# Stick-breaking attention: q and k projected with stationary weights, and the product for the second 512-key chunk on GpSimd

## The chip, the cores and the metric

The kernel runs on one core of one Trainium2 chip. The metric is the device time of one execution in microseconds. Engines are named as in the profile: PE is TensorE (PEld its weight loads), DVE VectorE, ACT ScalarE, POOL GpSimd, SP SyncE, whose queue issues nearly all transfers.

## What is computed

One block of a transformer trunk over 2048 positions of width 1024: RMS norm, one combined projection, two kinds of attention side by side (four heads of differential attention, eight heads of stick-breaking attention), an output projection with a residual, and a SwiGLU feed-forward part with a residual. The change is in stick-breaking attention alone:

```python
def stick_breaking_attention(q, k, v):
    """q, k, v: (B, S, H, D). A[t,s] = beta_ts * prod_{s<j<t}(1 - beta_tj), s < t."""
    ...
        z = jnp.einsum('bqhd,bkhd->bhqk', qb, k).astype(jnp.float32) * scale
        mask = (k_pos[None, :] < q_pos[:, None])[None, None]
        log_1mb = jnp.where(mask, jax.nn.log_sigmoid(-z), 0.0)
        rem = lax.cumsum(log_1mb, axis=3, reverse=True) - log_1mb
        a = jnp.where(mask, jnp.exp(jax.nn.log_sigmoid(z) + rem), 0.0)
        return jnp.einsum('bhqk,bkhd->bqhd', a.astype(v.dtype), v)
```

Here S = 2048, a head has D = 64, and the inputs are float32. The kernel gets more than float16 precision out of float16 matmuls by splitting each operand into a high and a low part (hi = float16 of the value, lo = float16 of the rest) and adding the products hi·hi, hi·lo and lo·hi.

## The kernel before

**Stages.** The work is cut into eight groups g. Groups 0 to 3 are one differential head each (two maps), groups 4 to 7 two stick-breaking heads each (m = 0, 1). The projection of a group is a stream of 16 tiles of 128 positions; it is written out ahead of the group's attention, mixed into the attention of the group before (`advance` says how many tiles must have been written by which step). A scheduler then gives each engine a fixed order from a simulated timeline and priorities (`pri`); the projection's matmuls ("pm") have a lower one than scores and values. While the last group runs there is no projection left, and the output projection (L761) takes its place. After that comes the feed-forward part, which the change does not touch. Where a function can use one of several engines, `pick` takes the one with the least load noted so far (`note`).

**Projection of a tile** (`proj_tile`, L314). The normalized and transposed inputs xt of a tile are the stationary operand, 128 x 128 at a time, and 384 columns of weights are the moving one (128 for q, 128 for k, 128 for v): 8 blocks of the inner dimension x 3 products = 24 matmuls into one PSUM bank `pj`, of which there are two. xt is reloaded from memory for each group (L386).

**Evacuation** (`proj_out`, L334, by `split_psum`, L324). For a stick-breaking group, v and then q with k are read from the bank twice each, once for hi (ACT or DVE) and once for lo (DVE, L330). q and k are put into `st` with positions on the partitions and, for each head, hi beside lo: 64 + 64 columns.

**Transposes** (`proj_batch`, L348). After four tiles two transposing transfers bring q and k to the layout that the scores need, with the inner dimension on the partitions (L372), and two plain transfers (L374) write a second copy of q with hi and lo swapped. All are on SP's queue. On the partitions of k then lie hi and lo of one head, 64 each.

**Scores** (`score_chunk`, L446). A row block i of 128 queries is scored against chunks of up to 512 keys. As hi and lo of k fill the 128 partitions together, two matmuls give all products: one with q in the swapped order, one with q in the straight order. At the diagonal a third, narrow one adds the mask (L450). There are four PSUM banks `sc`.

**Stick-breaking** (`stage_a`, L540). A unit is (i, m, b), b a block of up to 1024 keys, taken from the last key backwards. For each of its one or two chunks (c = 1 first, then c = 0): ACT makes 1 - beta into `om` (L554) and beta in place in the PSUM bank (L555), DVE runs the product scan backwards over `om` (L557) and multiplies beta by the scan shifted by one into `be` (L558). The buffers `om` and `be` are two of nine `z4`. After the unit `split_t` (L398) makes hi by a cast on ACT (L89) and lo by a subtraction on POOL (L98) into one of three `s16` buffers, and a transposing transfer on SP (L403) brings them to `aT`.

**Values** (`stage_b`, L565, `pv`, L453). Five units later PE multiplies aT by v, 64 columns a matmul (L458, three products per block of keys), into `yp`; `finish` normalizes, transposes and stores two or four row blocks at a time.

Of the kernel before, what the change touches and what calls it, by code (L numbers as in the profile page):

```python
# [11 lines left out]
F32 = mybir.dt.float32  # L12
F16 = mybir.dt.float16
# [46 lines left out]
def block(tc, a, out):  # L60
# [3 lines left out]
    with top:  # L64
# [30 lines left out]
        def tt(dst, a_, b_, op, n, engines="DP"):  # L95
            cost = {"D": 1.15 * n + 70, "P": 2.45 * n + 80}
            e = pick(**{k: cost[k] for k in engines})
            (DVE if e == "D" else POOL).tensor_tensor(dst, a_, b_, op)  # L98
# [10 lines left out]
        def nm(s):  # L109
            uid[0] += 1  # L110
            return f"{s}{uid[0]}"
# [13 lines left out]
        POOL.affine_select(tri[:], tri[:], pattern=[[-1, P]], compare_op=ALU.is_gt, fill=HIDDEN, base=0, channel_multiplier=1)  # L125
        mhalf = c1(16, "mh")
        DVE.memset(mhalf[:], -0.5)

        def times(o, a_, b_, c=None):
            DVE.tensor_scalar(o[:], a_[:], b_[:], c, op0=ALU.mult, **({} if c is None else {"op1": ALU.mult}))  # L130
# [120 lines left out]
        with ExitStack() as ph1:  # L251
# [62 lines left out]
            def proj_tile(G, xt):  # L314
# [6 lines left out]
                        n += 1  # L321
                return pj

            def split_psum(hi, lo, src, n):  # L324
                sc = 2.0 ** -11
                if pick(A=0.84 * n + 60, D=1.05 * n + 70) == "A":
                    ACT.mul(hi, src, sc)
                else:
                    DVE.tensor_scalar(hi, src, sc, None, op0=ALU.mult)
                DVE.scalar_tensor_tensor(lo, src, sc, hi, op0=ALU.mult, op1=ALU.subtract)  # L330
                note("D", 1.05 * n + 70)

            @pri("po")
            def proj_out(g, G, pj, B, j):  # L334
                st, v, raw = B
                nv = 1 if g < 4 else 2
                vv = v[:, j, :].rearrange("p (h s e) -> p h s e", h=nv, s=2)
                split_psum(vv[:, :, 0, :], vv[:, :, 1, :], pj[:, 256:384].rearrange("p (h e) -> p h e", h=nv), 128)
                if g < 4:
                    if pick(A=270, D=335) == "A":  # L340
                        ACT.mul(raw[:, j, :], pj[:, :256], 2.0 ** -11)
                    else:
                        DVE.tensor_scalar(raw[:, j, :], pj[:, :256], 2.0 ** -11, None, op0=ALU.mult)
                else:
                    split_psum(st[:, 0:4, j, 0, :], st[:, 0:4, j, 1, :], pj[:, :256].rearrange("p (c e) -> p c e", c=4), 256)

            @pri("pb")
            def proj_batch(g, G, B):  # L348
                st, v, raw = B
                qT = sp.tile([P, 4, 4, P], F16, tag="qT", bufs=QB, name=nm("qT"))  # L350
                kT = sp.tile([P, 2, 4, P], F16, tag="kT", bufs=KB, name=nm("kT"))
                if g < 4:
                    rq = raw[:].rearrange("p t (c e) -> p t c e", e=64)
                    sq = st[:].rearrange("p c t s e -> p (c t s e)")[:, :2048].bitcast(F32)
                    ACT.activation(sq.rearrange("p (t c e) -> p t c e", t=4, c=4), rq, AF.Square)
                    note("A", 950)
                    ss = sm.tile([P, 16], F32, tag="ss", bufs=2, name=nm("ss"))
                    DVE.tensor_reduce(ss[:], sq.rearrange("p (c e) -> p c e", e=64), op=ALU.add, axis=AX.X)
                    rs = sm.tile([P, 16], F32, tag="rs", bufs=2, name=nm("rs"))
                    rstd(rs[:], ss[:], 2.0 ** -16 / 64, G["epsk"][:])  # L360
                    rsb = rs[:].rearrange("p (t c) -> p t c", c=4).unsqueeze(3).to_broadcast([P, 4, 4, 64])
                    DVE.tensor_tensor(rq, rq, rsb, ALU.mult)
                    note("D", 2300)
                    gb = gk[:].unsqueeze(1).unsqueeze(1).to_broadcast([P, 4, 2, 64])
                    tt(rq[:, :, 2:4, :], rq[:, :, 2:4, :], gb, ALU.mult, 512)
                    for o in range(2):
                        src = rq[:, :, 2 * o : 2 * o + 2, :]
                        d = st[:, 2 * o : 2 * o + 2].rearrange("p c t s e -> p t c s e")
                        to16(d[:, :, :, 0, :], src, 512)
                        tt(d[:, :, :, 1, :], src, d[:, :, :, 0, :], ALU.subtract, 512)  # L370
                for T, c in ((qT[:, 2:4], 0), (kT[:], 2)):
                    SP.dma_start_transpose(T.rearrange("p c t n -> p (c t) n"), st[:, c : c + 2].rearrange("p c t s e -> p (c t s e)"))  # L372
                for o in (0, 64):
                    SP.dma_start(qT[o : o + 64, 0:2].rearrange("p c t n -> p (c t n)"), qT[64 - o : 128 - o, 2:4].rearrange("p c t n -> p (c t n)"))  # L374
                G["q"].append(qT)
                G["k"].append(kT)
                G["v"].append(v)

            def proj(g, G, fresh=None):
                for t in range(NT):  # L380
                    if fresh is not None:
                        feed(t)
                        xt = ahead.pop(0)
                    else:
                        xt = pp.tile([P, 2 * D], F16, tag="xt", bufs=3, name=nm("xt"))
                        SP.dma_start(xt[:], xs[t])  # L386
                    if t % 4 == 0:
                        st = pp.tile([P, 4, 4, 2, 64], F16, tag="st", name=nm("st"))
                        v = sp.tile([P, 4, 256], F16, tag="v", bufs=KB, name=nm("v"))
                        raw = pp.tile([P, 4, 256], F32, tag="raw", name=nm("raw")) if g < 4 else None  # L390
# [52 lines left out]
                return (i % k, k)  # L443

            @pri("sc")
            def score_chunk(G, sc, i, q, m, w, cut=False):  # L446
                for o in range(2):
                    PE.matmul(sc[:, : 128 * w].rearrange("p (t n) -> p t n", n=P), lhsT=G["q"][i // 4][:, 2 - 2 * o + m, i % 4, :], rhs=G["k"][q][:, m, 0:w, :], start=o == 0, stop=o == 1)  # L448
                if cut:
                    PE.matmul(sc[:, 128 * w - P : 128 * w], lhsT=idb[:], rhs=tri[:], start=False, stop=True, skip_group_check=True)  # L450

# [84 lines left out]
            def sb_attn(g, G):  # L536
                last = {}

                @pri("at")
                def stage_a(i, m, b):  # L540
                    L = (i + 1) * 128
                    n = min(1024, L - 1024 * b)
                    be, om = z4(), z4()
                    if b == i // 8:
                        DVE.memset(om[:, n : n + 1], 8192.0)
                    else:
                        DVE.tensor_copy(om[:, n : n + 1], last[m][:, 0:1])
                    last[m] = om
                    for c in range((n - 1) // 512, -1, -1):
                        lo, hi = 512 * c, min(512 * c + 512, n)  # L550
                        w = hi - lo
                        sc = ps.tile([P, 512], F32, tag="sc", bufs=4, name=nm("sc"))
                        score_chunk(G, sc, i, 2 * b + c, m, w // P, b == i // 8 and hi == n)
                        ACT.activation(om[:, lo:hi], sc[:, :w], AF.Sigmoid, scale=G["nkz"][:])  # L554
                        ACT.activation(sc[:, :w], sc[:, :w], AF.Sigmoid, scale=G["kz"][:])  # L555
                        ov = om[:, lo:hi][:, ::-1]
                        DVE.tensor_tensor_scan(ov, ov, sc[:, :w], om[:, hi : hi + 1], op0=ALU.mult, op1=ALU.bypass)  # L557
                        DVE.tensor_tensor(be[:, lo:hi], sc[:, :w], om[:, lo + 1 : hi + 1], ALU.mult)  # L558
                        note("A", 1.7 * w + 400)
                        note("D", 3.15 * w + 350)  # L560
                    return n, split_t(be[:, :n], n, "A", "P")

                ypd = {}
# [664 lines left out]
```

## Time and profile before

| | us |
|---|---|
| median of 3 runs (2730.43 to 2737.0) | 2735.74 |
| the profiled execution, its own time | 2740.3 |
| span of the profiled execution | 2738.5 |

In the profile a row of a group shows the line, the engine, the operation, the tile written and those read, the shape, the number of instructions, then busy time in us and the mean duration of one in ns, then the idle time of the engine just before them and what ended it. A row with "(+3 forms)" mixes shapes. A row of the order of time shows the start and the length of a piece of merged instructions, and xN counts them. Busy time is the union of the instructions' intervals, so for pipelined matmuls the mean of one is longer than busy time divided by the count. In a row of waits stand the total, the number of times and the longest wait. A row by window shows, for each engine, busy us and instructions, then the clock that TensorE was granted (1.0 is full speed), the busy share of the DMA engines and the rate. A DMA issue's row ends with its size and the median time to landing.

### The profile page before, as it was taken

What the parts mean: (1) busy time and instruction counts of PE and PEld (TensorE: products, weight loads), DVE (VectorE), ACT (ScalarE), POOL (GpSimd) and SP (SyncE); (2) the same over time, 40 slices, a digit from 0 to 9 for tenths busy, and PEclk for the clock granted to TensorE, in tenths of its full rate; (3) what the DMA queues carried; (4) which work ended last, traced back from release to release, by engine and by line L of the source; (5) the groups of instructions that cost most, each with busy time, mean ns of one, the idle gap of its engine ahead of it and who ended that gap; (6) DMA issues with size and microseconds to landing.
All of it is one profiled execution on the core that took longest, in us unless ns stands there. A gap on an engine that the chain in (4) does not pass through costs nothing.

```text
span 2738.5 us, 45414 instructions
## 1 busy us (share of the span) xinstructions
PE 2490.0 (91%) x17084; PEld 1409.8 (51%) x17084; DVE 1978.5 (72%) x3752; ACT 1353.3 (49%) x2539; POOL 1429.8 (52%) x1002
## 2 busy tenths in 40 slices
PE   7998989898978886889989898999999999999999
PEld 4655656565545553457775444444444444444444
DVE  6888879888888989987766777777786544434434
ACT  4665656566868778765644534344342212121121
POOL 2577677765554545546655566565664332222322
PEclk9999999998999997899999999999999999999999
DMA  6788787789998997997896665566657845635532
GB/s 227 199 164 178 151 198 164 180 171 200 208 201 184 212 186 151 203 192 208 213 289 256 220 234 191 208 221 216 231 204 283 316 158 181 220 128 193 192 116 93
DMA packets 646830, 543.52 MB, mean 198 GB/s; under 512 B 506369, under 2 KB 573953, under 8 KB 636369
## 3 DMA queue, kind: packets, MB, share of 16 engines
q1 hardware_dynamic: 644784, 538.53, 71.8%
q8 instruction: 134, 2.20, 0.3%
q0 software_dynamic: 512, 1.36, 0.2%
q10 hardware_dynamic: 1312, 0.72, 0.1%
q14 instruction: 88, 0.71, 0.1%
HBM read 261.08 MB, written 147.32 MB: 149 GB/s over the span
## 4 chain that ended last, share of the span: by engine, by line
PE 36%; DVE 9%; DMA 4%; POOL 3%; issue 3%; ACT 2%; SPq 0%; DVEq 0%; POOLq 0%; ACTq 0%
PE pd L1034 14%; PE pm L934 7%; PE pd L934 5%; PE pa L934 5%; DVE wd L215 2%; PE po L761 2%; DMA stages<-in_w_down_dram 1%; POOL stages L98 1%; DVE wu L215 1%; DMA aT<-s 1%; DVE z L557 1%; DVE cg L999 1%; DVE cg L98 1%; POOL s L98 1%; PE pj L320 1%
## 5 line engine op out<-in xcount | busy, mean ns | idle before, releaser
L98 POOL TENSOR_TENSOR s<-z,s 128x1024 f16<-128x1024 f32 (+7 forms) x288 | 474.4, 1655 | 320.1 <-ACT s L89 281.4
L320 PE MATMUL pj<-w,xt 128*128 128x384 f16 x3072 | 577.0, 336 | 19.2 <-DMA xt<-xs 5.6
L320 PEld LDWEIGHTS <-xt 128*128 128x128 f16 x3072 | 301.5, 101 | 233.1 <-issue 36.1
L557 DVE TENSOR_TENSOR_SCAN z<-z,sc 128x512 f32<-128x512 f32 (+3 forms) x320 | 356.1, 1114 | 72.1 <-ACT sc L555 68.8
L448 PE MATMUL sc<-kT,qT 128*128 128x512 f16 (+3 forms) x1280 | 348.3, 364 | 59.4 <-DVE z L558 23.7
L1034 PE MATMUL pd<-wd,act 128*128 128x512 f16 x1764 | 394.0, 381 | 7.2 <-DVE cu L968 7.1
L458 PE MATMUL yp<-v,aT 128*128 128x64 f16 (+1 forms) x4896 | 281.5, 209 | 82.3 <-DMA aT<-s 81.7
L458 PEld LDWEIGHTS <-aT 128*128 128x128 f16 x4896 | 245.4, 102 | 172.1 <-DMA aT<-s 110.4
L934 PEld LDWEIGHTS <-wg 128*128 128x128 f16 x1848 | 181.8, 98 | 228.1 <-issue 14.6
L934 PEld LDWEIGHTS <-wu 128*128 128x128 f16 x1848 | 180.8, 98 | 216.5 <-issue 2.0
L98 POOL TENSOR_TENSOR act<-cg,act 128x512 f16<-128x512 f32 x109 | 149.8, 1385 | 262.3 <-ACT act L993 262.3
L1034 PEld LDWEIGHTS <-act 128*128 128x128 f16 x1764 | 173.0, 98 | 216.6 <-issue 10.2
L89 ACT CAST s<-z 128x128 f16<-128x128 f32 (+7 forms) x216 | 170.3, 790 | 154.8 <-DMA aT<-s 72.9
L98 POOL TENSOR_TENSOR stages<-stages 128x512 f32<-128x512 f32 x97 | 172.9, 1783 | 120.1 <-DVE wg L215 41.4
L98 POOL TENSOR_TENSOR hs<-hs,cu 128x512 f32<-128x512 f32 x102 | 132.6, 1306 | 165.6 <-DVE hs L1040 62.7
L554 ACT ACTIVATE z<-sc,c 128x512 f32<-128x512 f32 (+3 forms) x320 | 204.4, 639 | 23.7 <-PE sc L448 18.9
L558 DVE TENSOR_TENSOR z<-sc,z 128x512 f32<-128x512 f32 (+3 forms) x320 | 193.7, 606 | 8.5
L555 ACT ACTIVATE sc<-sc,c 128x512 f32<-128x512 f32 (+3 forms) x320 | 196.5, 614 | 0.0
L1040 DVE SCALAR_TENSOR_TENSOR hs<-pd,c,hs 128x512 f32<-128x512 f32 x144 | 106.5, 748 | 118.5 <-PE pd L1034 113.6
L761 PE MATMUL po<-wo,mt 128*128 128x256 f16 x1536 | 180.7, 275 | 12.3 <-DVE xf L764 6.8
L993 ACT CAST act<-cg 128x512 f16<-128x512 f32 x126 | 76.9, 616 | 231.4 <-DVE cg L999 192.7
L934 PE MATMUL pm<-X,wu 128*128 128x512 f16 x792 | 179.1, 379 | 1.8 <-ACT cg L979 1.7
(241 smaller groups left out, 4109.1 us busy)
## 6 DMA issues: line engine op xcount, KB each, us to landing
xt<-xs SPq DMA_DIRECT2D x112, 512.0 KB, 4.4
hs<-hd SPq DMA_DIRECT2D x72, 512.0 KB, 4.5
hd<-hs SPq DMA_DIRECT2D x56, 512.0 KB, 5.8
split<-wg SPq DMA_DIRECT2D x11, 1792.0 KB, 6.9
split<-wu SPq DMA_DIRECT2D x11, 1792.0 KB, 6.7
split<-wd SPq DMA_DIRECT2D x11, 1792.0 KB, 6.8
wg<-split SPq DMA_DIRECT2D x11, 1792.0 KB, 7.4
wd<-split SPq DMA_DIRECT2D x11, 1792.0 KB, 9.1
```

The source lines that it names most:

```text
L89: ACT.copy(dst, src)
L98: (DVE if e == "D" else POOL).tensor_tensor(dst, a_, b_, op)
L320: PE.matmul(pj[:, :384], lhsT=xv[:, xi, kt, :], rhs=G["w"][:, wi, kt, :], start=n == 0, stop=n == 23)
L448: PE.matmul(sc[:, : 128 * w].rearrange("p (t n) -> p t n", n=P), lhsT=G["q"][i // 4][:, 2 - 2 * o + m, i % 4, :], rhs=G["k"][q][:, m, 0:w, ...
L458: PE.matmul(yp[:, y0 : y0 + wd], lhsT=aT[:, a_, :], rhs=v[:, v_ : v_ + wd], start=start and j == 0 and q == 0, stop=stop and j == nb - 1 a ...
L554: ACT.activation(om[:, lo:hi], sc[:, :w], AF.Sigmoid, scale=G["nkz"][:])
L555: ACT.activation(sc[:, :w], sc[:, :w], AF.Sigmoid, scale=G["kz"][:])
L557: DVE.tensor_tensor_scan(ov, ov, sc[:, :w], om[:, hi : hi + 1], op0=ALU.mult, op1=ALU.bypass)
L558: DVE.tensor_tensor(be[:, lo:hi], sc[:, :w], om[:, lo + 1 : hi + 1], ALU.mult)
L761: PE.matmul(po[:, sl], lhsT=mt[:, kt, P * xi : P * xi + P], rhs=wos[2 * h + n][wi][:, kt, :], start=q == 0, stop=q == 23)
L934: PE.matmul(ps_[:].rearrange("p (t n) -> p t n", n=P), lhsT=wv[:, wo, wi, 128 * kt : 128 * kt + 128], rhs=X[xo][:, :, xi, kt, :], start=st ...
L1034: PE.matmul(po[:], lhsT=act[:, ao, xi, 128 * j : 128 * j + 128], rhs=W["d"][:, wo, wi, :], start=start and u == 0 and q == 0, stop=u == nu ...
```

## The change

**Projection.** For groups 4 to 7, `proj_turned` takes the place of `proj_tile`. For q and for k the weights are the stationary operand and 128 positions of xt the moving one, so that q and k come out with the inner dimension on the partitions; v is made as before, alone. That is 72 matmuls of 128 columns for each tile. Two tiles share two banks: q (256 columns) and k (256) of both in one, v of both in the other. `turned_out` then reads the banks once for the pair. On the partitions now lie the 64 dimensions of head 0 and the 64 of head 1. For each head, q is multiplied by a column `half` that is 2^-11 on that head's partitions and zero on the other's: hi by ACT, lo by DVE. k is split once for both heads. `st`, the transposing transfers of q and k and the swapped copies are no longer used in these groups; in `proj_batch` the differential groups' work is unchanged.

**Scores.** With hi and lo in separate tiles, a chunk of stick-breaking takes three matmuls: hi·hi, lo·hi, hi·lo. Half of the rows of the stationary operand (q) are zero in each.

**Product.** In the chunk c = 1, beta is written to `be` in SBUF instead of back into the PSUM bank, and the product with the scan is done on POOL, in place in `be`. The scan's second operand there is the raw score bank; the scan passes it by. Chunk c = 0 and units with one chunk are as before. The notes of load for `pick` follow.

```diff
+        half = c1(2, "half")
+        DVE.memset(half[:], 0.0)
+        for m in range(2):
+            DVE.memset(half[64 * m : 64 * m + 64, m : m + 1], 2.0 ** -11)
...
+            @pri("pm")
+            def proj_turned(G, xt, pq, pv, r):
+                xv = xt[:].rearrange("p (s k n) -> p s k n", s=2, k=KT)
+                for c in range(3):
+                    n = 0
+                    for kt in range(KT):
+                        for xi, wi in ((0, 0), (0, 1), (1, 0)):
+                            w_, x_ = G["w"][:, wi, kt, 128 * c : 128 * c + 128], xv[:, xi, kt, :]
+                            o = pv[:, P * r : P * r + P] if c == 2 else pq[:, 256 * c + P * r : 256 * c + P * r + P]
+                            PE.matmul(o, lhsT=x_ if c == 2 else w_, rhs=w_ if c == 2 else x_, start=n == 0, stop=n == 23)
+                            n += 1
+
+            @pri("po")
+            def turned_out(pq, pv, qT, kT, v, j):
+                two = slice(j - 1, j + 1)
+                q2, k2 = (pq[:, 256 * c : 256 * c + 256].rearrange("p (t n) -> p t n", t=2) for c in range(2))
+                for m in range(2):
+                    ACT.mul(qT[:, m, two, :], q2, half[:, m : m + 1])
+                    DVE.scalar_tensor_tensor(qT[:, 2 + m, two, :], q2, half[:, m : m + 1], qT[:, m, two, :], op0=ALU.mult, op1=ALU.subtract)
+                note("A", 800)
+                note("D", 800)
+                split_psum(kT[:, 0, two, :], kT[:, 1, two, :], k2, 256)
+                vv = v[:, two, :].rearrange("p t (h s e) -> p t h s e", h=2, s=2)
+                split_psum(vv[:, :, :, 0, :], vv[:, :, :, 1, :], pv[:, :256].rearrange("p (t h e) -> p t h e", t=2, h=2), 256)
...
+                    if g >= 4:
+                        if t % 4 == 0:
+                            qT, kT = new_qk()
+                            G["q"].append(qT)
+                            G["k"].append(kT)
+                            G["v"].append(v)
+                        if t % 2 == 0:
+                            pq, pv_ = (psj.tile([P, 512], F32, tag="pj", name=nm("pj")) for _ in range(2))
+                        proj_turned(G, xt, pq, pv_, t % 2)
+                        if t % 2 == 1:
+                            turned_out(pq, pv_, qT, kT, v, t % 4)
+                        yield
+                        continue
...
-            def score_chunk(G, sc, i, q, m, w, cut=False):
-                for o in range(2):
-                    PE.matmul(sc[:, : 128 * w].rearrange("p (t n) -> p t n", n=P), lhsT=G["q"][i // 4][:, 2 - 2 * o + m, i % 4, :], rhs=G["k"][q][:, m, 0:w, :], start=o == 0, stop=o == 1)
+            def score_chunk(G, sc, i, q, m, w, cut=False, turned=False):
+                terms = ((m, 0), (2 + m, 0), (m, 1)) if turned else ((2 + m, m), (m, m))
+                for o, (a_, b_) in enumerate(terms):
+                    PE.matmul(sc[:, : 128 * w].rearrange("p (t n) -> p t n", n=P), lhsT=G["q"][i // 4][:, a_, i % 4, :], rhs=G["k"][q][:, b_, 0:w, :], start=o == 0, stop=o == len(terms) - 1)
...
-                        score_chunk(G, sc, i, 2 * b + c, m, w // P, b == i // 8 and hi == n)
+                        score_chunk(G, sc, i, 2 * b + c, m, w // P, b == i // 8 and hi == n, True)
+                        aside = c == 1
+                        beta = be[:, lo:hi] if aside else sc[:, :w]
                         ACT.activation(om[:, lo:hi], sc[:, :w], AF.Sigmoid, scale=G["nkz"][:])
-                        ACT.activation(sc[:, :w], sc[:, :w], AF.Sigmoid, scale=G["kz"][:])
+                        ACT.activation(beta, sc[:, :w], AF.Sigmoid, scale=G["kz"][:])
                         ov = om[:, lo:hi][:, ::-1]
                         DVE.tensor_tensor_scan(ov, ov, sc[:, :w], om[:, hi : hi + 1], op0=ALU.mult, op1=ALU.bypass)
-                        DVE.tensor_tensor(be[:, lo:hi], sc[:, :w], om[:, lo + 1 : hi + 1], ALU.mult)
+                        (POOL if aside else DVE).tensor_tensor(be[:, lo:hi], beta, om[:, lo + 1 : hi + 1], ALU.mult)
                         note("A", 1.7 * w + 400)
-                        note("D", 3.15 * w + 350)
+                        note("D", 2.1 * w + 150)
+                        note("P" if aside else "D", (1.65 if aside else 1.05) * w + 100)
```

More of the change, by code (lines that the diff above doesn't have):

```diff
@@ L335, in proj_out, with new_qk @@
                 st, v, raw = B
[L336 to L343, printed above, removed]
-                else:
-                    split_psum(st[:, 0:4, j, 0, :], st[:, 0:4, j, 1, :], pj[:, :256].rearrange("p (c e) -> p c e", c=4), 256)
+                vv = v[:, j, :].rearrange("p (s e) -> p s e", s=2)
+                split_psum(vv[:, 0, :], vv[:, 1, :], pj[:, 256:384], 128)
+                if pick(A=270, D=335) == "A":
+                    ACT.mul(raw[:, j, :], pj[:, :256], 2.0 ** -11)
+                else:
+                    DVE.tensor_scalar(raw[:, j, :], pj[:, :256], 2.0 ** -11, None, op0=ALU.mult)
+            def new_qk():
+                qT = sp.tile([P, 4, 4, P], F16, tag="qT", bufs=QB, name=nm("qT"))
+                kT = sp.tile([P, 2, 4, P], F16, tag="kT", bufs=KB, name=nm("kT"))
+                return qT, kT
             @pri("pb")
@@ L349, in proj_batch @@
                 st, v, raw = B
[L350 to L365, printed above, removed]
-                    for o in range(2):
[L367 to L370, printed above, removed]
@@ new lines, in proj_batch @@
+                qT, kT = new_qk()
+                rq = raw[:].rearrange("p t (c e) -> p t c e", e=64)
+                sq = st[:].rearrange("p c t s e -> p (c t s e)")[:, :2048].bitcast(F32)
+                ACT.activation(sq.rearrange("p (t c e) -> p t c e", t=4, c=4), rq, AF.Square)
+                note("A", 950)
+                ss = sm.tile([P, 16], F32, tag="ss", bufs=2, name=nm("ss"))
+                DVE.tensor_reduce(ss[:], sq.rearrange("p (c e) -> p c e", e=64), op=ALU.add, axis=AX.X)
@@ new lines, in proj_batch @@
+                rs = sm.tile([P, 16], F32, tag="rs", bufs=2, name=nm("rs"))
+                rstd(rs[:], ss[:], 2.0 ** -16 / 64, G["epsk"][:])
+                rsb = rs[:].rearrange("p (t c) -> p t c", c=4).unsqueeze(3).to_broadcast([P, 4, 4, 64])
+                DVE.tensor_tensor(rq, rq, rsb, ALU.mult)
+                note("D", 2300)
+                gb = gk[:].unsqueeze(1).unsqueeze(1).to_broadcast([P, 4, 2, 64])
+                tt(rq[:, :, 2:4, :], rq[:, :, 2:4, :], gb, ALU.mult, 512)
+                for o in range(2):
+                    src = rq[:, :, 2 * o : 2 * o + 2, :]
+                    d = st[:, 2 * o : 2 * o + 2].rearrange("p c t s e -> p t c s e")
+                    to16(d[:, :, :, 0, :], src, 512)
+                    tt(d[:, :, :, 1, :], src, d[:, :, :, 0, :], ALU.subtract, 512)
@@ L387, in proj @@
                     if t % 4 == 0:
+                        v = sp.tile([P, 4, 256], F16, tag="v", bufs=KB, name=nm("v"))
+                    if g >= 4:
+                        if t % 4 == 0:
+                            qT, kT = new_qk()
+                            G["q"].append(qT)
[8 more added lines that the diff above has]
+                        continue
+                    if t % 4 == 0:
                         st = pp.tile([P, 4, 4, 2, 64], F16, tag="st", name=nm("st"))
-                        v = sp.tile([P, 4, 256], F16, tag="v", bufs=KB, name=nm("v"))
-                        raw = pp.tile([P, 4, 256], F32, tag="raw", name=nm("raw")) if g < 4 else None
+                        raw = pp.tile([P, 4, 256], F32, tag="raw", name=nm("raw"))
                     pj = proj_tile(G, xt)
```

1 line of the change is left out of this document (removed).

## The prediction, made before the changed kernel was run

> **What bounds the kernel now.** I read the page first, then the stages (busy time in three windows), then the waits, the DMA issues and the groups of the window that the change works in, and last the order of time for rates.
>
> The page, parts 1 and 2:
>
> ```profile
> span 2738.5 us, 45414 instructions
> ...
> PE 2490.0 (91%) x17084; PEld 1409.8 (51%) x17084; DVE 1978.5 (72%) x3752; ACT 1353.3 (49%) x2539; POOL 1429.8 (52%) x1002
> ...
> PEclk9999999998999997899999999999999999999999
> DMA  6788787789998997997896665566657845635532
> ```
>
> Over the whole span PE looks like the bound at 91%. The clock row and the DMA row say that one stretch is different: about slices 9 to 17 (68 us each) the granted clock dips and the DMA engines are at 9 tenths. That stretch is stick-breaking. By windows (the end of differential attention; stick-breaking with projections beside it; the last group with the output projection beside it):
>
> ```profile
> core 0: us, PE busy (x) PEld busy (x) DVE busy (x) ACT busy (x) POOL busy (x), PEclk, DMA share, GB/s
> 460.00:605.00 145.00, 131.40 (x1053) 84.25 (x1051) 128.81 (x372) 83.91 (x216) 100.79 (x72) 0.98 0.79 173
> 605.00:1180.00 575.00, 469.06 (x4723) 291.95 (x4720) 515.59 (x927) 454.40 (x877) 301.44 (x194) 0.90 0.96 192
> 1180.00:1390.00 210.00, 187.54 (x1973) 151.99 (x1974) 154.97 (x250) 126.84 (x222) 121.55 (x83) 0.98 0.86 209
> ```
>
> In 605 to 1180 PE is busy 82% at a clock of 0.90, DVE 90%, the DMA engines 96%, ACT 79%, POOL 52%. So VectorE and the transfers set the pace there, and PE waits. In 1180 to 1390 PE is at 89% and DVE at 74%. The waits of 605 to 1180 name the same two:
>
> ```profile
> POOL s L98 <- ACT s L89: 224.3, 105, 7.2
> ...
> PE yp L458 <- DMA aT<-s: 47.4, 43, 2.9
> ACT s L89 <- DMA aT<-s: 45.3, 36, 3.9
> DVE z L557 <- ACT sc L555: 39.7, 47, 4.6
> ...
> PE sc L448 <- DVE z L558: 22.3, 24, 2.4
> ```
>
> The transposes of the probabilities (aT) hold PE directly, and hold ACT through the three s16 buffers; ACT stands in order, so a cast that waits for a transpose delays the sigmoids behind it, and the scan waits for those. DVE's own multiply (L558) holds the score buffers. POOL's 224 us are slack: it waits for ACT.
>
> **Part 1, the transfers that go.** The issues of that window, and four pieces of SP's order of time:
>
> ```profile
> q1 hardware_dynamic: 292204, 109.73, 95.1%
> ...
> qT<-qT SPq DMA_DIRECT2D x26, 128.0 KB, 2.6
> ...
> aT<-s SPq DMA_TRANSPOSE x162, 4.4
> ...
> qT<-st SPq DMA_TRANSPOSE x13, 3.3
> kT<-st SPq DMA_TRANSPOSE x13, 3.6
> ```
>
> ```profile
> 910.61 1.37 SPq L372 DMA_TRANSPOSE qT<-st  x1
> 912.03 1.33 SPq L372 DMA_TRANSPOSE kT<-st  x1
> 913.96 0.47 SPq L374 DMA_DIRECT2D qT<-qT  x1
> ...
> 917.40 1.12 SPq L374 DMA_DIRECT2D qT<-qT  x1
> ...
> 955.25 26.48 SPq L403 DMA_TRANSPOSE aT<-s  x11
> ```
>
> Eleven aT transposes keep SP for 26.48 us, 2.4 us each: SP's queue is a resource too. One batch of q and k costs it 1.37 + 1.33 + 0.47 + 1.12 = 4.3 us, thirteen of them 56 us of the 575. In blocks of 128x128, the q/k batches are 16 blocks x 16 = 256, the aT of eight heads 2 x 136 x 8 = 2176, so 10.5% of the transposed blocks go. If the transfers were the only limit and all their time were transposes, 575 would fall to 575 x 0.895 = 515; if the transposes are hidden, to 575. Nothing replaces them: q and k come out of PE already transposed, and their swap is not needed.
>
> **Part 2, VectorE.** The groups of 605 to 1180 that the change touches:
>
> ```profile
> L557 DVE TENSOR_TENSOR_SCAN z<-z,sc 128x512 f32<-128x512 f32 (+3 forms) x263 | 289.8, 1103 | 42.6 <-ACT sc L555 39.7
> ...
> L320 PE MATMUL pj<-w,xt 128*128 128x384 f16 x1286 | 243.6, 340 | 5.4 <-DMA xt<-xs 2.8 <-DVE st L330 1.9 <-DVE m L178 0.7
> ...
> L558 DVE TENSOR_TENSOR z<-sc,z 128x512 f32<-128x512 f32 (+3 forms) x262 | 157.2, 601 | 7.3
> L448 PE MATMUL sc<-kT,qT 128*128 128x512 f16 (+3 forms) x524 | 152.1, 379 | 48.8 <-DVE z L558 22.3 <-DVE z L545 15.2 <-DVE z L547 8.7
> L458 PE MATMUL yp<-v,aT 128*128 128x64 f16 (+1 forms) x2729 | 131.7, 203 | 47.8 <-DMA aT<-s 47.4 <-DVE mo L436 0.2
> L320 PEld LDWEIGHTS <-xt 128*128 128x128 f16 x1286 | 126.5, 102 | 95.9 <-issue 17.8 <-DMA xt<-xs 5.1 <-DVE st L330 1.0
> ```
>
> A head scores 136 x 128 = 17,408 columns; the second chunk (c == 1) has 1280 (rows 4 to 7) + 8 x 512 + 1280 (second block) = 6656 of them, 38.2%, in 128 of 320 multiplies. Of the 157.2 us of L558, 60 us leave DVE. In that chunk the scan no longer waits for the second sigmoid, which now writes be. Added is the evacuation of q in two masked copies:
>
> ```profile
> L330 DVE SCALAR_TENSOR_TENSOR st<-pj,st 128x256 f16<-128x256 f32 x53 | 21.4, 408 | 2.9 <-ACT st L327 2.9
> ...
> L330 DVE SCALAR_TENSOR_TENSOR v<-pj,v 128x128 f16<-128x128 f32 x54 | 14.5, 274 | 0.4 <-ACT v L327 0.3
> ...
> L327 ACT ACTIVATE st<-pj 128x256 f16<-128x256 f32 x54 | 21.0, 395 | 13.7 <-DVE v L330 13.4 <-PE sc L450 0.3
> ...
> L327 ACT ACTIVATE v<-pj 128x128 f16<-128x128 f32 x54 | 15.7, 296 | 1.2 <-PE pj L320 1.1
> ```
>
> Two tiles cost DVE 2 x (408 + 274) = 1.36 us now and 4 x 408 = 1.63 us after; ACT 1.38 and 1.58 us. Over 27 pairs that is +7 us DVE and +5 us ACT. DVE: 515.6 - 60 + 7 = 463 us, which at its present 90% needs 516 us. ACT: 459, not the bound.
>
> **Part 3, GpSimd.** The trace has no such product on POOL here; the nearest rows are subtractions of the same size from SBUF (the second from the feed-forward part):
>
> ```profile
> L98 POOL TENSOR_TENSOR z<-z 128x512 f32<-128x512 f32 x11 | 14.4, 1311 | 6.4 <-ACT z L782 6.0
> ```
>
> ```profile
> L98 POOL TENSOR_TENSOR stages<-stages 128x512 f32<-128x512 f32 x97 | 172.9, 1783 | 120.1 <-DVE wg L215 41.4 <-DVE wd L215 34.1 <-DVE wu L215 31.0
> ```
>
> At 1311 ns per 512 columns, 53,248 columns cost 136 us, at 1783 ns 185 us. I take the first: same buffers, same stage. Some 82% falls into 605 to 1180 (262 of 320): 301 + 112 = 413 us, about 74% of the stage. The cover: POOL multiplies chunk 1 while DVE scans and multiplies chunk 0 (for 512 columns about 1.10 + 0.60 us by the means above), so the cast that needs both chunks waits for POOL only when POOL is in an earlier subtract. Behind the waiting product on POOL stand the subtracts that release aT; without cover each product puts 1.3 us ahead of an aT.
>
> **Part 4, PE.** Rates from the order of time (first three lines: differential stage; the fourth stick-breaking) and from the chain of waits:
>
> ```profile
> 206.52 0.22 PE L458 MATMUL yp<-v,aT 128*128 128x128 f16 x1
> ...
> 209.11 1.22 PE L458 MATMUL yp<-v,aT 128*128 128x128 f16 x19
> ...
> 210.44 4.06 PE L320 MATMUL pj<-w,xt 128*128 128x384 f16 x24
> ...
> 859.84 0.95 PE L458 MATMUL yp<-v,aT 128*128 128x64 f16 x27
> ...
> 1460.43 2.59 PE pm L934 x12
> ```
>
> A single 128-column matmul takes 0.22 us from end to end, so in the run of 19 each further one, with weights of its own, took (1.22 - 0.22) / 18 = 55.5 ns. For 384 columns I take 256 columns more for the single one, at 216 ns per 512 (2.59 us for 12): 0.33 us, and (4.06 - 0.33) / 23 = 162 ns each. A tile's projection goes from 24 x 162 = 3.89 to 72 x 55.5 = 4.00 us: +0.11 us, 6 us over 54 tiles. Bounds: nothing, or, if each matmul had to wait for its weight load (102 ns mean), 72 x 102 - 3890 = +3.5 us a tile.
>
> The Trainium skill, "TensorE: Matmul & The Clock Gate", section "Back-to-back issue gap", speaks against this change: it gives about 81 ns per matmul of 128 columns, sustained, in a stream of weight load and matmul pairs. By that figure a tile would go to 5.83 us instead of 4.00, and my sum would be 99 us higher. The trace's run of 19 at 55.5 ns does not bear it out, and its 512-column matmuls (216 ns) do not fit the 131 ns beside it.
>
> The third score term is a full one: half of the stationary rows are zero, and PE pays for columns. 17,408 x 8 columns x 216 / 512 ns = 58.7 us; 524 of 640 score matmuls are in the stage, so 48 us there and 11 us after. Streamed at these rates the stage's PE work is now 208 (L320) + 96 (L448, two terms) + 96 (L458, 35 ns each with its tail) + about 12 (masks, small transposes; estimate) = 412 us, after it 466. Busy time scales to 469 x 466 / 412 = 530 us at a clock of 0.90, or 487 at the 0.98 that stages with a busier PE were granted. At the 91% of the window 460 to 605 that needs 535 us (clock 0.98) to 582 us (0.90).
>
> **The sum.** In 605 to 1180 the limits afterwards are 516 (DVE), 515 to 575 (transfers), 535 to 582 (PE): PE is late next. I take 555, a little below the middle of PE's ends, because the clock follows PE's busy share from window to window: -20 us. In 1180 to 1390 PE gets 11 us more at 89%, DVE some 14 us less at 74%: between 0 and +11, I take +3, since DVE's waits for PE are only part of that stretch. Before 605 the first stick-breaking projection runs beside differential attention: PE +1 us, a few transposes fewer, taken at nothing, covered by a PE that is busy 91% either way. After 1390 nothing changes. 2740.3 us (the profiled execution; its span is 2738.5) - 17 = 2723.3; that execution lies 4.6 us above the median of 2735.7, so 2719.
>
> **Rivals.**
> - *Pairs without a second buffer* (slower). q/k and v of two tiles fill both pj banks, so the next pair cannot start before turned_out has read them: four evacuations of 395 ns and a last 408 ns, 2.0 us at least, where one tile now evacuates while the next is multiplied (PE waited 1.9 us in all for L330). Unless scores and values fill that gap, 27 pairs x 2 us = 54 us; with 17 us gained, 2719 + 54 = 2773. It decides from about 0.6 us of unfilled wait a pair (17 / 27). For it: in-order ACT and DVE evacuate late. Against: PE has 200 us of other work in the stage.
> - *PE paces the stage already* (slower): its 106 us of idle time stay, and 48 + 6 + 11 us of new work come on top: 2736 + 65 = 2801. Against it: DVE 90% and DMA 96% busy.
> - *The weight load holds each 128-column matmul* (slower): +3.5 us x 54 = 189 us in place of 6, 2902 at most. The run of 19 is against it. The Trainium skill's 81 ns on the page named above would give 2818.
> - *What DVE sheds comes back on POOL* (no change): products ahead of subtracts delay aT by as much as DVE gains, 20 us: 2736 +- 8. For it: aT is what PE and ACT wait for.
>
> **How the numbers follow.** A measurement here tells about 0.3% (8 us) from no change. The forecast gets 0.53 (own range 2690 to 2727, the stage at 535 to 565), no change 0.12, pairs 0.22 (2744 to 2785), PE pacing 0.09, weight loads 0.04. So faster 0.53, same 0.12, slower 0.35. 2685 to 2785 leaves out PE pacing, the weight loads and a tail of the first and third.
>
> **What would show it.** Right: the transposes from st and the copies qT to qT gone; q/k matmuls at 56 ns in a run; L558 on DVE near 120 us and some 136 us of new POOL products; DVE in the stick-breaking stage near 83%, PE near 90%, a clock above 0.93, aT waits shorter. Wrong: PE idle before the projections, released by the evacuation; POOL above 85% with transposes waiting for it; runs of 128-column matmuls at 80 ns or more; or a stage longer than 575 us.

## The result, and the profile after

The changed kernel takes 2745.8 us (median of 8, 2742.8 to 2750.46), the kernel before 2736.37 (8 runs, 2730.28 to 2741.37): ratio 1.0039, 95% interval 1.0027 to 1.0051. It is slower by some 11 us, where 17 us less was forecast; the profiled execution took 2750.46 us. Ratios below are to the kernel before on the same chip; for sums I turn them into us with 2735, so 1.0039 is +11.

The page after, its instruction totals, clock and DMA rows:

```profile
span 2748.7 us, 52197 instructions
...
PE 2524.9 (92%) x20476; PEld 1543.2 (56%) x20476; DVE 1955.7 (71%) x3686; ACT 1353.0 (49%) x2494; POOL 1521.2 (55%) x1116
...
PEclk9999999999999999999999999999999999999999
DMA  6778687777888979886797665665657845535532
```

The dip of the clock is gone, the DMA row has fallen from 9 to 8 tenths in stick-breaking, PE has 35 us more and POOL 91 us more. DVE has only 23 us less. By windows, before and then after, from about the first scan to the last projection matmul, and from there to the last matmul of the output projection:

```profile
605.00:1200.00 595.00, 486.60 (x4878) 302.69 (x4876) 527.70 (x955) 463.15 (x900) 307.72 (x199) 0.90 0.96 194
1200.00:1458.00 258.00, 230.98 (x2382) 194.70 (x2380) 178.82 (x281) 140.22 (x227) 152.13 (x101) 0.98 0.88 242
```

```profile
609.00:1220.00 611.00, 526.84 (x8122) 429.63 (x8123) 527.49 (x927) 482.53 (x893) 416.73 (x319) 0.97 0.85 176
1220.00:1469.00 249.00, 224.62 (x2274) 191.04 (x2270) 160.17 (x239) 118.87 (x188) 134.76 (x96) 0.99 0.81 231
```

The columns are those of the prediction's table: length, busy us of PE, PEld, DVE, ACT and POOL, then clock and DMA share. The stage that should have shrunk by 20 us grew by 16; 3 to 4 us were lost before it, and the last stretch gave 9 back. PE was busy 40 us longer in the stage, and its idle time fell from 108 to 84 us. In the stage nothing is full any more: PE 86%, DVE 86%, ACT 79%, POOL 68%, DMA 85%. Its waits (609 to 1220):

```profile
POOL s L98 <- ACT s L89: 88.9, 71, 5.0
POOL z L604 <- DVE z L603: 85.9, 63, 5.9
PE yp L502 <- DMA aT<-s: 48.1, 41, 3.7
ACT s L89 <- DMA aT<-s: 38.2, 28, 2.8
DVE z L603 <- ACT sc L601: 32.6, 35, 3.4
DVE z L603 <- ACT z L601: 15.4, 13, 4.1
```

PE waits for aT as long as before (47.4 us then). DVE still waits 48 us for the second sigmoid (44 before, 605 to 1200), by the profile's account in chunk 1 too (L601 writing z), although the scan does not use what that writes. The groups that the change made, over the same stage:

```profile
L338 PE MATMUL pj<-xt,w 128*128 128x128 f16 x2784 | 221.5, 224 | 9.9 <-DVE v L360 5.4 <-DVE m L183 2.9 <-DVE z L589 1.5
L492 PE MATMUL sc<-kT,qT 128*128 128x512 f16 (+3 forms) x846 | 204.5, 355 | 20.8 <-DVE z L589 6.4 <-DVE z L604 6.0 <-ACT v L357 2.4
...
L502 PE MATMUL yp<-v,aT 128*128 128x64 f16 (+1 forms) x2911 | 141.6, 196 | 49.4 <-DMA aT<-s 48.1 <-DVE mo L479 1.0
...
L338 PE MATMUL pj<-w,xt 128*128 128x128 f16 x1385 | 129.2, 220 | 0.0
...
L604 DVE TENSOR_TENSOR z<-sc,z 128x512 f32<-128x512 f32 (+3 forms) x173 | 105.1, 609 | 4.6
L604 POOL TENSOR_TENSOR z<-z,z 128x512 f32<-128x512 f32 (+3 forms) x110 | 104.6, 952 | 92.3 <-DVE z L603 85.9 <-DVE c L175 2.3 <-DVE z L589 1.9
```

The first row of L338 is q and k, the second v. The scores took 155 us of the stage before (605 to 1200) and take 205 now; the projections hardly wait for their banks (10 us, of which 5.4 for an evacuation, L360). And the rates, from PE's order of time:

```profile
902.75 2.84 PE L338 MATMUL pj<-xt,w 128*128 128x128 f16 x48
905.43 1.46 PE L492 MATMUL sc<-kT,qT 128*128 128x512 f16 x6
...
908.96 0.81 PE L492 MATMUL sc<-kT,qT 128*128 128x512 f16 x3
909.61 0.25 PE L502 MATMUL yp<-v,aT 128*128 128x64 f16 x3
```

The run of 48 projection matmuls took (2.84 - 0.22) / 47 = 55.7 ns for each. Three score matmuls hold PE 0.65 us, 216 ns each.

### The profile page after: what moved, and what is told of

Read it like the earlier page. It is cut to its first block, busy times and chain, and to the rows that moved or that the text cites. A ratio compares the mean times of both kernels' runs of the same rounds, so it can differ in the third digit from the quotient of the medians.

```text
span 2748.7 us, 52197 instructions
## 1 busy us (share of the span) xinstructions
PE 2524.9 (92%) x20476; PEld 1543.2 (56%) x20476; DVE 1955.7 (71%) x3686; ACT 1353.0 (49%) x2494; POOL 1521.2 (55%) x1116
## 5 line engine op out<-in xcount | busy, mean ns | idle before, releaser
L98 POOL TENSOR_TENSOR s<-z,s 128x1024 f16<-128x1024 f32 (+7 forms) x288 | 468.0, 1634 | 117.9 <-ACT s L89 106.7
L492 PE MATMUL sc<-kT,qT 128*128 128x512 f16 (+3 forms) x1600 | 400.1, 355 | 32.4 <-DVE z L589 6.4
L502 PE MATMUL yp<-v,aT 128*128 128x64 f16 (+1 forms) x4896 | 281.1, 205 | 82.7 <-DMA aT<-s 81.2
L502 PEld LDWEIGHTS <-aT 128*128 128x128 f16 x4896 | 241.7, 100 | 151.9 <-DMA aT<-s 100.8
L325 PE MATMUL pj<-w,xt 128*128 128x384 f16 x1536 | 288.1, 334 | 13.3 <-ACT raw L369 5.5
L338 PE MATMUL pj<-xt,w 128*128 128x128 f16 x3072 | 244.3, 223 | 10.0 <-DVE v L360 5.4
L89 ACT CAST s<-z 128x128 f16<-128x128 f32 (+7 forms) x215 | 170.5, 797 | 122.6 <-DMA aT<-s 59.9
L338 PEld LDWEIGHTS <-w 128*128 128x128 f16 x3072 | 209.0, 100 | 30.9 <-DVE v L360 6.6
L325 PEld LDWEIGHTS <-xt 128*128 128x128 f16 x1536 | 151.4, 100 | 119.7 <-issue 18.2
L604 POOL TENSOR_TENSOR z<-z,z 128x512 f32<-128x512 f32 (+3 forms) x128 | 122.8, 960 | 130.7 <-DVE z L603 124.3
L492 PEld LDWEIGHTS <-qT 128*128 128x128 f16 x1600 | 135.4, 100 | 99.7 <-issue 17.2
```

Of the source, the lines that this page charges most:

```text
L89: ACT.copy(dst, src)
L325: PE.matmul(pj[:, :384], lhsT=xv[:, xi, kt, :], rhs=G["w"][:, wi, kt, :], start=n == 0, stop=n == 23)
L338: PE.matmul(o, lhsT=x_ if c == 2 else w_, rhs=w_ if c == 2 else x_, start=n == 0, stop=n == 23)
L502: PE.matmul(yp[:, y0 : y0 + wd], lhsT=aT[:, a_, :], rhs=v[:, v_ : v_ + wd], start=start and j == 0 and q == 0, stop=stop and j == nb - 1 a ...
L604: (POOL if aside else DVE).tensor_tensor(be[:, lo:hi], beta, om[:, lo + 1 : hi + 1], ALU.mult)
```

## The experiments

**The two halves apart, and three suspects.** *e1* is the changed kernel with `aside = False`, so that all products stay on DVE; *e2* is the kernel before with the lines of the product alone; *e3* leaves out one score term, so its scores are less precise; *e4* gives each tile one bank again.

```diff
e1  -  aside = c == 1
    +  aside = False
e3  -  terms = ((m, 0), (2 + m, 0), (m, 1)) if turned else ...
    +  terms = ((m, 0), (2 + m, 0)) if turned else ...
e4  -  pq, pv_ = (psj.tile(...) for _ in range(2))      # at every second tile
    +  pj = psj.tile(...)                               # at every tile, turned_out after it
```

> The turned projection and the third score term alone; all products stay on VectorE. If the new TensorE work is what ate the gain (theory PE), this is clearly slower than the changed kernel, whose product on GpSimd then pays some of it back: 2755 to 2775 us. If the product on GpSimd is itself the loss (theory POOL), this is faster than the changed kernel and than before: 2715 to 2735. If the missing second bank is the loss (theory banks), about as the changed kernel or a little slower, 2746 to 2765.

> The product of the second chunk on GpSimd alone, with the projection and the two-term scores of before. Theory PE: VectorE's 75 us of work gone and no new TensorE work, so clearly faster than before, 2700 to 2720. Theory POOL: no gain or a loss, 2735 to 2760. Theory banks says nothing beyond theory PE here: 2700 to 2720.

> The changed kernel without the third score term (the product of the high part of q and the low part of k is left out, so the scores are less precise). It takes away 59 us of TensorE time, 48 of them in the stick-breaking stage. Theory PE: 2746 falls by 20 to 45 us, to 2700 to 2726. Theories banks and POOL: little, 2738 to 2746.

> The changed kernel with one bank for q, k and v of a tile, as before, so that one tile is evacuated (eight instructions of 128 columns) while the next is multiplied. Theory banks: the projections no longer wait, 2715 to 2735. Theories PE and POOL: no gain, and twice as many short evacuations on ScalarE and VectorE (about +15 us of each over the run), 2746 to 2760.

Measured: e1 2771.07 us, ratio 1.0114 (1.0095 to 1.0132), +31. e2 2726.92, 0.9968 (0.9957 to 0.9979), -9. e3 2719.76, 0.9936 (0.9918 to 0.9954), -18. e4 2764.48, 1.0093 (1.0077 to 1.011), +25. The product on GpSimd gains, though e2 stays above the range that theory PE gave it; the turned projection with its third term loses 31 us alone; without that term the change is 28 us faster and beats the kernel before. A bank for each tile is 15 us worse than the pairs. That run also has twice as many evacuations, but PE's 10 us of waits for the banks leave the pairs no large part of the loss. The stage of e3 (first scan to last projection):

```profile
609.00:1190.00 581.00, 481.74 (x7771) 405.41 (x7769) 514.40 (x911) 472.30 (x879) 417.41 (x314) 0.95 0.88 183
```

30 us shorter than that of the changed kernel, with 45 us less of PE.

**TensorE's work put into the kernel before.** Matmuls with a stationary operand of zeros add to PE's load and leave the values as they are. In the stick-breaking groups there is one more for each score chunk (*e6*), six more for each projection tile (*e10*), a narrow one (*e14*) and two wide ones (*e15*) for each chunk. They do not change the load alone: the scheduler makes each engine's order anew. In e6, ACT runs two casts (L89) one after the other at 626.29 and then copies q and k (L327); before, the copy at 631.01 stood between the two casts.

```diff
e6    PE.matmul(sc[...], lhsT=<q>, rhs=<k>, start=o == 0, stop=...)      # o = 0, 1
      +  PE.matmul(sc[...], lhsT=id16[:], rhs=G["k"][q][:, m, 0:w, :], start=False, stop=True)   # id16 is zero
e10   +  if n % 4 == 2: PE.matmul(pj[:, :384], lhsT=id16[:], rhs=G["w"][:, wi, kt, :], start=False, stop=False)
e14   +  if o == 0: PE.matmul(sc[:, :P], lhsT=id16[:], rhs=G["k"][q][:, m, 0, :], start=False, stop=False)
```

> The kernel before with a third score matmul for each stick-breaking chunk whose stationary operand is zero: TensorE gets the same 59 us, nothing else changes. Theory PE (the third term costs its time wherever it stands, about 26 us by the run without it): 2736 + 20 to 40, so 2756 to 2776. Theory cover (TensorE's waits in the stage before hide it, and it only costs in the changed kernel, where VectorE and the transfers are relieved): 2736 to 2748.

> The kernel before with six more matmuls of 384 columns and a zero stationary operand in each tile of the stick-breaking projections: 6 x 64 x 162 ns = 62 us of TensorE, as much as the zero term in the scores (59 us, +28), but not on the way from a score to its sigmoid and none of it after the last projection. If any work on TensorE costs about half its time in this stage (theory throughput): 2736 + 20 to 35. If the zero term cost because each score comes later (theory score path): 2736 to 2746.

> The kernel before with a zero score matmul of 128 columns for each stick-breaking chunk: 320 x 55.5 ns = 18 us of TensorE, 14 to 15 us of them in the stage. Theory bound (TensorE's work is free until TensorE is the last of several limits, as the prediction took it): no change, 2735 +- 5. Theory share (each us of TensorE costs about half from the first, since no engine alone sets the pace): +8 to +10, 2743 to 2746.

> The kernel before with two zero score matmuls of the chunk's width: 117 us of TensorE, 96 in the stage. Theory bound: the first 28 us came at 59; beyond the point where TensorE is the limit each further us costs a whole one, so +28 + 59 = +87, 2822. Theory share: about +56, 2791; in between if the share grows as TensorE fills up.

| | PE work added, us | ratio (interval) | us | PE idle in the stage, us (before: 108) |
|---|---|---|---|---|
| e14 | 18 | 1.0030 (1.0017 to 1.0043) | +8 | 107 |
| e6 | 59 | 1.0104 (1.0089 to 1.0119) | +28 | 102 |
| e10 | 62 | 1.0136 (1.0115 to 1.0156) | +37 | 99 |
| e15 | 117 | 1.0119 (1.0102 to 1.0136) | +33 | 76 |

The third term costs the same 28 us in the kernel before (e6) as in the changed one (2746 - 2720 = 26 by the medians, 1.0039 - 0.9936 = 28 by the ratios). It is not the later score: as much work in the projections costs at least as much (e10). A limit that is reached only at some point does not fit either, as the first 18 us cost 8. How much of each step is PE's work and how much the new order was not separated; a step of 8 us could be order alone, but the 28 us come out both when the term is added and when it is taken away, in two different orders. The second 59 us of e15 cost only 5 more, which neither theory expected. The stages of before, e14, e6 and e15 stand at 0.90 (above) and:

```profile
605.00:1202.00 597.00, 490.45 (x5095) 312.60 (x5093) 524.73 (x942) 460.14 (x895) 304.39 (x197) 0.93 0.95 190
```

```profile
605.00:1210.00 605.00, 502.91 (x5088) 312.60 (x5086) 523.88 (x939) 459.30 (x890) 304.67 (x196) 0.96 0.92 187
```

```profile
605.00:1230.00 625.00, 548.82 (x5411) 341.72 (x5408) 531.31 (x952) 465.72 (x899) 302.37 (x199) 0.98 0.91 185
```

PE's busy share goes from 82 through 82 and 83 to 88%, the clock from 0.90 through 0.93 and 0.96 to 0.98, and DVE's work stays within 8 us. In these profiles the second step is not small in the stage itself: e6 ends it 10 us later than the kernel before, e15 another 20. Of the 62 us that PE is busy longer in e15, 32 came out of its idle time. The stretch after the stage is 258 us before, 269 in e6 and 262 in e15. Why it grows less in e15, so that the whole comes to 33 us, is open.

**Are the transfers the other limit?** In *e7* (the kernel before) and *e8* (e2) groups 5 to 7 take q and k from group 4, so their scores are not those of the reference.

```diff
      def proj_batch(g, G, B):
+         if g > 4:
+             G["q"], G["k"] = Gs[4]["q"], Gs[4]["k"]
+             G["v"].append(v)
+             return
```

> The kernel before, but groups 5 to 7 take q and k of group 4, so that 24 of the 32 pairs of transposing transfers and swapped copies go (other values than the reference's; the projections and evacuations of these groups are still done). Theory transfers (they are a limit beside VectorE, which still stands): 5 to 15 us faster, 2721 to 2731. Theory hidden: no change, 2730 to 2742.

> The same with the second chunk's product on GpSimd (again groups 5 to 7 use q and k of group 4). The product alone gave 10 us, and in that run the DMA engines were at 97% in the stage and ScalarE waited 72 us for transposes. Theory transfers: with them relieved the product gives its full 25 us, as it does on the turned projection: 2695 to 2708. Theory hidden: 2727, as with the product alone.

e7: 2724.34 us, 0.9974 (0.9965 to 0.9984), -7. e8: 2707.86, 0.9915 (0.9900 to 0.9931), -23, which is 7 more than -7 and -9 together; with the intervals that is between 1 and 13 us. In e2, with the transfers at 97%, this is the row of ACT's wait for transposes (605 to 1175), beside 45.3 us before:

```profile
ACT s L89 <- DMA aT<-s: 70.9, 47, 4.9
```

So in e2 ACT waited longer for transposes, and with three quarters of those of q and k gone the product gives more. That the one is the reason for the other is not shown: the stage took 570 us in e2's profile (605 to 1175) and 573 in e8's (605 to 1178, at 90% of the DMA engines), and e8's profile is the slowest of its six runs. Both reliefs that the prediction counted on exist.

**Cheaper forms of the turned projection.** *e9* keeps q of both heads in one tile and scores a head on its own 64 partitions; *e11* and *e12* go back to two terms with nothing left out, in that plain transfers put the low part of k under the high part, and the high part of q on both halves of the partitions.

```diff
e9    -  for m in range(2): ACT.mul(qT[:, m, two, :], q2, half[:, m : m + 1]) ...
      +  split_psum(qT[:, 0, two, :], qT[:, 1, two, :], q2, 256)        # scores: rows 64 * m : 64 * m + 64
e11   +  SP.dma_start(qT[hs[1 - m], m], qT[hs[m], m]); SP.dma_start(kT[hs[1 - m], m], qT[hs[m], 3])
      +  terms = ((hs[m], 2, m), (slice(0, P), m, m))                   # low part of q on 64 rows
e12   +  terms = ((2 + m, m), (m, m))                                   # low part of q masked, 128 rows
```

> The changed kernel with q evacuated once for both heads, without the masked copies; a head's score matmuls then use its own 64 partitions of q and k. It takes one of two hi and one of two lo evacuations of q away, about 14 us of ScalarE and 13 us of VectorE (500 and 464 ns by 28 each), and leaves the number and the columns of the matmuls. Theory PE: as many columns, so little, 2738 to 2746. If the evacuation of q is a good part of what the turned projection costs: 2725 to 2737. If TensorE runs matmuls on different halves of the rows beside each other, more: below 2725.

> The changed kernel with two score terms instead of three and nothing left out: the high part of q stands on both halves of the partitions, the high and the low part of k on one half each (four plain copies of 64 partitions a batch bring them there), and the low part of q meets the high part of k on 64 partitions. The product on GpSimd stays. Theory PE: as the run with two terms, less what the copies and two more evacuations a pair cost: 2717 to 2727, which would be below before and about the product on GpSimd alone. If the copies cost as the transposes did: 2727 to 2735.

> As the run with the stacked k, but the low part of q is a masked copy over all 128 partitions, so that both score matmuls have 128 rows. In the run before, a chunk's two matmuls held TensorE 0.54 us, not 0.43, before the next could start, which two matmuls of equal rows did not. If that change of rows (320 x 0.11 = 35 us of TensorE) was what ate the gain of the dropped term: about half of it comes back, and with it most of the term's 28 us: 2720 to 2735. If it is the evacuation in halves (five pairs of copies instead of four for two tiles) and the order that follows from it: still above the changed kernel, 2746 to 2775.

e9: 2738.09 us, 1.0028 (1.0013 to 1.0043), +8, 3 less than the changed kernel, which is within the intervals. e11: 2777.54, 1.0144 (1.0123 to 1.0165), +39. e12: 2750.27, 1.0059 (1.0039 to 1.0078), +16. In e9 the three terms hold PE 0.75 us before the next matmul of 128 rows starts, not 0.65 as above:

```profile
904.06 0.82 PE L489 MATMUL sc<-kT,qT 64*128 64x512 f16 x3
904.81 0.20 PE L499 MATMUL yp<-v,aT 128*128 128x64 f16 x1
```

In e11 the two terms hold it 0.55 us, where two of equal rows take 0.43:

```profile
911.96 0.71 PE L496 MATMUL sc<-kT,qT 64*128 64x512 f16 x2
912.51 1.39 PE L338 MATMUL pj<-xt,w 128*128 128x128 f16 x22
```

Over e9's 320 chunks that is 32 us of PE. In the stage of e9 (607 to 1217) PE is busy 567 of 610 us, 93%, which is 40 us more than in the changed kernel, while DVE and ACT have 12 and 16 us less, and the stage is as long as there. In this run PE's waits covered the new work, with less load on the engines that it waits for. The change of rows is likely part of e11's loss, as e12 without it is 23 us better. Neither brings the gain of the dropped term: e11 lies some 40 us above its ranges, and e12 lies in the range that was given for the case that the evacuation in halves and the new order are the cause, slower than the changed kernel though it has 59 us less of score matmuls. Four plain copies a batch that wait on SP for evacuations, more evacuations a pair, and another order: which of them costs this was not separated.

**The planner's answer, and the best version.** The page's 23 us less of DVE are few: 76 us of products left it (L558 193.7 us before, L604 118.1 now). The high copies of the projections on DVE (L359) went from 0.3 us to 19.0, as the noted load fell, and the low copies of q take 465 ns where 408 was reckoned. *e16* and *e17* put all high copies on ACT (`pick(A=...)` alone), in the changed kernel and in e2; *e13* is e2 once more.

> The changed kernel with every high part of the projections copied by ScalarE. As the load noted on VectorE fell, the planner moved 45 of these copies to it (0.3 us of VectorE before, 19.0 us after). Theory planner (what the product took off VectorE was given back there): 3 to 10 us faster than the changed kernel, 2736 to 2743. Theory share, with ScalarE as an in-order engine that counts as much: no gain or a loss, 2744 to 2752.

> The same in the kernel with only the product on GpSimd, where 25.5 us of high copies went to VectorE. Theory planner: 2715 to 2723 against 2727. Theory share: 2725 to 2733.

> The product of the second chunk on GpSimd alone, once more beside the run above, as the fastest version that leaves nothing out: 0.9957 to 0.9979 of the kernel before, 2724 to 2730.

e16: 2755.14 us, 1.0079 (1.0064 to 1.0093), +22. e17: 2731.25, 0.9997 (0.9989 to 1.0006), -1. e13: 2728.55, 0.9977 (0.9964 to 0.9990), -6. e16 lies above both of its ranges. So the move was no loss: undone, it costs 11 us, and 8 against e2 (5 against e13). That suggests that ACT is as much on the way as DVE. The product alone (e2, e13) is the fastest version that leaves nothing out, and beats both kernels.

## Why the prediction was wrong

**The step that failed** is in the sum: "At the 91% of the window 460 to 605", and with it "PE is late next. I take 555". It took the stage as the largest of three limits and let PE's waits cover the new PE work until PE would be 91% busy. Measured: PE's busy time came out as reckoned (next paragraph), but PE stood idle for 84 of the stage's 611 us, 14%, where 9% was assumed; its wait for aT, which was to get shorter, stayed (47.4 us, then 48.1). Of 40 us more busy time 24 were covered and 16 made the stage longer. Over the whole run the third term alone costs 28 us for 59 us of matmul columns, in e6 as in e3. My reading is that DVE, ACT, PE and the transfers, at 79 to 86% in this stage and each engine in a fixed order, wait for each other in turn, so that PE's waits are only in part free cover; no run shows that by itself.

That e3 came out at -18 where the sum said -17 is luck. The sum had priced the third term. Without its 48 us the same sum has PE at 418 us of streaming, 476 us busy at a clock of 0.90 and 523 us at 91%, beside 516 for DVE, so a stage well below 555. The stage of e3 took 581 us, with PE at 83% and DVE at 89%: the step fails there too.

**The clock** rose as expected, 0.90 to 0.97, and the price of PE's work was right. The 527 us of busy time stand for more work than the sum's 466 us of streaming, as the stage measured to the last projection has 2784 + 1385 projection matmuls (58 tiles, not 54), 846 score matmuls and 2911 of L502. At the sum's rates that is 231 + 155 + 102 + 12 = 500 us, and 527 / 500 = 1.05 at a clock of 0.97, where the kernel before had 469 / 412 = 1.14 at 0.90. For 466 us it gives 491, next to the forecast's 487 at 0.98. PE's busy share alone does not set the clock: at 82 to 83% busy it was 0.90 (before), 0.93 (e14), 0.95 (e3) and 0.96 (e6).

**Right, or nearly.** The projection in 72 narrow matmuls: 55.5 ns forecast, 55.7 measured, and the rival in which the weight loads hold the matmuls falls with that. The Trainium skill, "TensorE: Matmul & The Clock Gate", section "Back-to-back issue gap", gives about 81 ns for a sustained stream of weight loads and matmuls of 128 columns; the run of 48 does not bear it out. GpSimd's products: 136 us forecast, 123 over the run by the profile's page, with 68% busy for 74% forecast. Transfers: with fewer of them e7 gains 7 us. Wrong: the last stretch, +3 forecast, was 9 us shorter in the profile, and the time before the first scan, taken at nothing, was 3 to 4 us longer.

**DVE** was to lose 53 us in the stage and stands at some 527 us as before (605 to 1200, 609 to 1220). The products took 55 us from it. The evacuations put 30 us back where 7 were reckoned, some 18 of them high copies that the planner moved there, and the longer stage holds 14 more scans (14 us). e16 shows that the high copies were not the loss; the rest was not tried.

**The rivals.** Pairs without a second buffer: against it that the projections waited only 10 us for their banks, and e4, as far as its additional evacuations allow. No change by POOL: against it e2, and the changed kernel against e1 (-20 us for the product). "PE paces the stage already" comes nearest to the cause, with the wrong size: of its 65 us the turned projection with the third term cost 31 (e1), and it left out the product's gain.

## What to carry to other kernels

Where a stage has four resources at 80 to 96% and fixed instruction orders, do not take its time as the largest of their limits. Here added PE work cost 0.3 to 0.6 of its length, although PE waited a fifth of the time, and moving 19 us of copies from DVE to ACT cost 11 us. Count matmul columns before transfers: one more full-width term for each chunk cost 28 us, while three quarters of the transposes of q and k and 76 us of VectorE's products together brought 23. And measure the halves of a two-part change apart: here one gains 6 to 9 us alone and 20 us beside the other, which loses 31. Remember that each edit also gives the scheduler a new order, whose share of a few us no single run separates.

## What was not expected of the hardware

Matmuls of 64 rows between matmuls of 128 rows cost 0.10 us a change and back (0.75 for 0.65 us for three of 512 columns; 0.55 for 0.43 for two in e11). The median of 200 such groups of three in e9's trace is 0.75 us, of 190 in the changed kernel's 0.65. A second zero term of 59 us cost 5 us over the run where the first cost 28, with the granted clock at 0.98 in that stage instead of 0.96; in the stage itself, by one profile of each, it cost 20 us where the first cost 10.
